# A SwiGLU FFN in seven block products: the gate of a second 1024 columns by the scheme, its up columns plain and turned

## The chip, the cores and the metric

The kernel runs on one core of a Trainium2 chip. The metric is the device time of one execution in microseconds (us), the median of several runs.

## The reference

One decoder block on 256 tokens of width 1024: a gated linear recurrence and a block-sparse attention side by side, gated, summed and projected, and then a dense SwiGLU FFN with `D_FF` = 2816. All arrays are float32. The change lies almost wholly in the last line:

```python
h2 = rmsnorm(x, ffn_norm_g[l])
x = x + (jax.nn.silu(h2 @ w_ffn_gate[l]) * (h2 @ w_ffn_up[l])) @ w_ffn_down[l]
```

`w_ffn_gate` and `w_ffn_up` are 1024 x 2816, `w_ffn_down` is 2816 x 1024. A small part of the change lies in the gate of the first branch, `sigmoid(h @ w_in[:, 7168:8192])`.

## The kernel before, in words

**Arithmetic.** Every float32 operand is split in two parts that TensorE can multiply: a high part, written by a cast on ScalarE (`whi`, line 55), and the rest, written by a subtraction on VectorE (`wlo`, line 56). One product of matrices is then three on TensorE: high by high, high by low, low by high. Weights come from memory in chunks of 1 MB (128 x 2048), each by one DMA on SyncE's queue (`load_w`, line 67, or `quarter`, line 631), and each chunk costs a cast and a subtraction of 128 x 2048. The pool `wp` that holds `wraw`, `whi` and `wlo` has three buffers of each, so the cast of a chunk can start only when TensorE has finished with the chunk three before it.

**Names.** Tokens are two blocks of 128 (index i); DFF is 22 tiles of 128 columns. `x2T` is the normalised input with the model dimension on the partitions, in high and low part. PSUM has eight banks under three tags: `pw` (4), `ph` (2), `pa` (2). In the code a quarter of a weight is `W11`, `W12`, `W21`, `W22`; in the rows below the same tiles count from zero, `W00`, `W01`, `W10`, `W11`, so that the code's `W11` is `W00` there and its `W22` is `W11`.

**Three ways to multiply by a weight.** The *plain, feature-major* way (`feat_steps`, lines 101 to 105) keeps weights stationary: for each tile of 128 columns and each of eight slices of the model dimension one matmul of 128x512 (weight's high part by high and low activations) and one of 128x256 (its low part). The sums of the two halves of a bank are then added by `fold` (ScalarE line 121, VectorE line 122). The result has the columns on the partitions, as the down projection needs it. The *token-major* way keeps the activations stationary and moves 512 columns: three matmuls of 128x512 for each slice and token block. The *scheme* (line 831) computes 2 x 2 blocks (tokens by columns, 512 deep) by seven block products instead of eight; a product (line 641) is 12 matmuls of 128x512. It needs the four quarters of a 1024 x 1024 weight, four sums of quarters (128 x 2048 each, on VectorE), sums of the activations (`token_sums2`, four arrays of 128x512, split in two pieces), and additions that put the products together. Its result is token-major, so it is turned by transposes on TensorE (`turn`, line 961: four transposes of 128x128 and a split of 128x512).

**The FFN before.** With `NPL` = 14, tiles 0 to 13 (three blocks of four and one of two) are plain and feature-major, for gate and up. Tiles 14 to 21, the last 1024 columns, go by the scheme, the gate between the chunks of the plain blocks and the up columns between the chunks of the down projection, one product and one down chunk in turn; `turn` runs four times. A down chunk (`down_steps`, lines 903 to 905) is 24 matmuls of 128x512 for two tiles; there are eleven, d0 to d10, and they add into four banks (`acc`).

**What sets the order.** The order of the steps is written out: `step` (line 795) lets nothing of a step be put ahead of the last matmul of the step before it, and a scheduler then fixes, at build time, the order on each engine. Each engine executes its own list in that order and waits at an instruction until what it needs is ready; nothing behind it overtakes.

Of the kernel before, what the change touches and what calls it, by code (L numbers as in the profile page):

```python
# [14 lines left out]
P = 128  # L15
# [12 lines left out]
def tile_hgrn2_moba_block(ctx: ExitStack, tc: tile.TileContext, xm, xw, table, runs,  # L28
# [672 lines left out]
    nc.scalar.copy(gq(1, 0), b1)  # L701
# [3 lines left out]
    at = then(product, b3, summed(0), halves(W11), True)  # L705
    W22 = quarter(1, 1, "T8")
# [16 lines left out]
    nc.vector.tensor_add(gq(1, 1), b2, gq(1, 0))
    nc.vector.tensor_add(gq(1, 1), gq(1, 1), b3)
# [55 lines left out]
    NPL = 14  # L780
    SC = NPL * P

    def token_sums2():
# [3 lines left out]
        nc.vector.tensor_add(C[:, 0], x2f[:, 0, :, P:S], x2f[:, 1, :, P:S])  # L787
        nc.vector.tensor_sub(C[:, 1], C[:, 0], x2f[:, 0, :, 0:P])
        nc.vector.tensor_sub(C[:, 2], x2f[:, 0, :, 0:P], x2f[:, 0, :, P:S])
        nc.vector.tensor_sub(C[:, 3], x2f[:, 1, :, 0:P], C[:, 1])  # L790
# [8 lines left out]
    def plain(f0, nf, b):  # L799
# [20 lines left out]
        hT = big.tile([P, nf, 2, S], F32R, name="hT", tag=("T7", "T2", "T3", "T12")[b])  # L820
# [6 lines left out]
        for j in range(nf):  # L827
            hk.append((f0 + j, hT, j))
        yield

    def scheme(w, banks, p1, at_out, q):

        X = x2T
        W11 = quarter(0, 0, "T10", w, SC)
        W21 = quarter(1, 0, "T9", w, SC)
        W12 = quarter(0, 1, "T11", w, SC)
        W22 = quarter(1, 1, "T8", w, SC)
        b1 = banks()
        product(b1, tokens(0, 0, X), halves(W11), True)
        nc.scalar.copy(p1, b1)  # L840
        nc.vector.tensor_sub(W11, W12, W11)
# [17 lines left out]
        nc.vector.tensor_sub(W21, W21, W11)
# [14 lines left out]
    def down_steps():  # L874
        (fa, act, ja), (fb, act_b, jb) = hk[2 * chunk[0]:2 * chunk[0] + 2]
        assert fb == fa + 1 and act is act_b
# [4 lines left out]
        for tb in range(2):  # L881
            for half in range(2):
                ts = slice(tb * P, (tb + 1) * P)
                cs = slice(half * 512, (half + 1) * 512)
                if end and tb == 1 and half == 1:
                    for c0, cw in ((512, 256), (768, 256)):
                        bank = pw()
                        for i in range(2):
# [10 lines left out]
                for i in range(2):  # L899
                    j = ja + i  # L900
                    st = n == 0 and i == 0
                    en = i == 1 and n == NFT // 2 - (2 if tb == 1 and half == 1 else 1)
                    nc.tensor.matmul(acc[tb][half], act[:, j, 0, ts], hi[:, i, cs], start=st, stop=False)  # L903
                    nc.tensor.matmul(acc[tb][half], act[:, j, 0, ts], lo[:, i, cs], start=False, stop=False)  # L904
                    tail[0] = nc.tensor.matmul(acc[tb][half], act[:, j, 1, ts], hi[:, i, cs], start=False, stop=en)  # L905
# [26 lines left out]
    third, chunk_no = None, 0
    for what in "cccsPcPccPcPccPcPcPc":
        if what == "c":
            with tc.issue_after(x2_split[0].ins), tc.issue_after(x2_split[1].ins):
                step(next, chunks_a) if chunk_no == 2 else None
            if chunk_no != 2:
                step(next, chunks_a)
            third = third or (halved[-1] if chunk_no == 2 else None)
            chunk_no += 1  # L940
            continue
# [106 lines left out]
```

## Time and profile before

| | |
|---|---|
| median of 3 runs | 490.17 us (490.13 to 490.63) |
| profiled execution | 490.14 us |
| its span | 488.4 us, so 1.74 us lie around it |
| TensorE busy | 483.1 us (99%), 2598 matmuls |
| VectorE busy | 397.8 us (81%), 426 instructions |
| ScalarE busy | 301.7 us (62%), 402 instructions |
| GpSimd busy | 25.2 us (5%), 59 instructions |
| granted TensorE clock | 1.00 |

The span is from the first to the last recorded instruction; the metric is somewhat longer. TensorE works almost without a gap, so its list of instructions is nearly the time. Where another engine's result comes later than TensorE's place in that list, a gap opens, and everything behind it moves. The FFN begins at about 305 us of the span.

### The profile page before, as it was taken

The numbers are of one execution on the slowest core, as the hardware profiler recorded it, in microseconds if no ns is written. First come the engines' busy times: TensorE is split into PE (matmuls) and PEld (weight loads), VectorE is DVE, ScalarE is ACT, GpSimd is POOL, SyncE is SP. The second block draws the span as 40 slices with busy tenths as digits, with TensorE's granted clock in tenths as the row PEclk, the third lists the DMA queues.
The fourth block names the chain that finished last, engine by engine and source line by source line (L and its number), as shares of the span: only waits on it lengthen the run. The fifth ranks groups of instructions, "written<-read, shape, count | busy, mean of one in ns | idle before, by whom it ended". The sixth has DMA issues, their size and how long they took to land.

```text
span 488.4 us, 6511 instructions
## 1 busy us (share of the span) xinstructions
PE 483.1 (99%) x2598; PEld 406.7 (83%) x2598; DVE 397.8 (81%) x426; ACT 301.7 (62%) x402; POOL 25.2 (5%) x59
## 2 busy tenths in 40 slices
PE   8999999999999999999999999999999999999997
PEld 7888888888888888988888878888888888888885
DVE  5769999697779989499987767899998779986843
ACT  5887656767748984875564445886566576444520
POOL 1930320000000000000000000000000000000000
PEclk9999999999999999999999999999999999999999
DMA  8977695624524348418267577715395664242402
GB/s 314 401 240 253 196 299 187 224 87 158 190 83 158 134 139 269 166 46 299 90 233 281 172 260 260 251 37 183 128 338 179 178 250 171 92 173 86 172 1 86
DMA packets 42142, 91.16 MB, mean 187 GB/s; under 512 B 1656, under 2 KB 3960, under 8 KB 42112
## 3 DMA queue, kind: packets, MB, share of 16 engines
q1 hardware_dynamic: 41376, 88.11, 52.5%
q0 software_dynamic: 736, 2.65, 1.7%
q8 instruction: 20, 0.33, 0.3%
q14 instruction: 10, 0.08, 0.1%
HBM read 89.67 MB, written 1.07 MB: 186 GB/s over the span
## 4 chain that ended last, share of the span: by engine, by line
PE 96%; DVE 2%; DMA 1%; issue 0%; ACT 0%
PE pw L102 16%; PE pw L84 10%; PE pw L85 10%; PE pw L86 10%; PE pw L168 5%; PE pw L105 4%; PE acc L903 4%; PE acc L905 4%; PE acc L904 4%; PE pw L101 4%; PE pw L645 4%; PE b L645 4%; PE g L645 3%; PE pw L684 1%; PE pw L685 1%; PE pw L683 1%
## 5 line engine op out<-in xcount | busy, mean ns | idle before, releaser
L56 DVE TENSOR_TENSOR wlo<-wraw,whi 128x2048 fp32r<-128x2048 f32 (+1 forms) x69 | 148.9, 2163 | 37.7 <-ACT whi L55 37.4
L55 ACT CAST whi<-wraw 128x2048 fp32r<-128x2048 f32 (+1 forms) x69 | 124.8, 1813 | 62.1 <-PE pw L86 25.2
L102 PE MATMUL pw<-x2T,whi 128*128 128x512 f32 x224 | 71.8, 395 | 0.0
L55 ACT CAST whi<-W 128x2048 fp32r<-128x2048 f32 x21 | 40.2, 1915 | 28.5 <-PE acc L905 13.6
L84 PE MATMUL pw<-whi,XT 128*128 128x512 f32 x144 | 56.9, 395 | 0.0
L56 DVE TENSOR_TENSOR wlo<-W,whi 128x2048 fp32r<-128x2048 f32 x21 | 47.9, 2286 | 10.2 <-ACT whi L55 10.1
L86 PE MATMUL pw<-whi,XT 128*128 128x512 f32 x144 | 56.2, 390 | 0.0
L85 PE MATMUL pw<-wlo,XT 128*128 128x512 f32 x144 | 56.1, 390 | 0.0
L102 PE MATMUL pw<-XT,whi 128*128 128x512 f32 x128 | 40.6, 395 | 0.0
L102 PEld LDWEIGHTS pw<-x2T,whi 128*128 128x128 f32 x224 | 35.0, 189 | 0.4
L86 PEld LDWEIGHTS pw<-whi,XT 128*128 128x128 f32 x144 | 27.0, 188 | 5.7
L84 PEld LDWEIGHTS pw<-whi,XT 128*128 128x128 f32 x144 | 27.0, 188 | 5.6
L105 PE MATMUL pw<-x2T,wlo 128*128 128x256 f32 x112 | 31.3, 279 | 0.3 <-DVE wlo L56 0.3
L85 PEld LDWEIGHTS pw<-wlo,XT 128*128 128x128 f32 x144 | 27.1, 188 | 5.4
L101 PE MATMUL pw<-x2T,wlo 128*128 128x256 f32 x112 | 31.2, 279 | 0.0
L105 PEld LDWEIGHTS pw<-x2T,wlo 128*128 128x128 f32 x112 | 21.1, 188 | 5.2 <-DVE wlo L56 0.7
L101 PEld LDWEIGHTS pw<-x2T,wlo 128*128 128x128 f32 x112 | 21.0, 188 | 5.0
L903 PE MATMUL acc<-whi,hT 128*128 128x512 f32 x56 | 21.9, 391 | 0.0
L905 PE MATMUL acc<-whi,hT 128*128 128x512 f32 x56 | 21.8, 390 | 0.0
L904 PE MATMUL acc<-wlo,hT 128*128 128x512 f32 x56 | 21.8, 389 | 0.0
L102 PEld LDWEIGHTS pw<-XT,whi 128*128 128x128 f32 x128 | 19.8, 189 | 0.2
L168 PE MATMUL pw<-whi,XT 128*128 128x512 f32 x64 | 17.6, 393 | 0.3 <-ACT whi L182 0.3
(357 smaller groups left out, 1019.9 us busy)
## 6 DMA issues: line engine op xcount, KB each, us to landing
wraw<-w_in SPq DMA_DIRECT2D x26, 1024.0 KB, 5.1
wraw<-w_down SPq DMA_DIRECT2D x11, 1024.0 KB, 5.0
wraw<-w_gate SPq DMA_DIRECT2D x6, 1024.0 KB, 5.1
wraw<-w_up SPq DMA_DIRECT2D x6, 1024.0 KB, 5.1
wraw<-w_at SPq DMA_DIRECT2D x4, 1024.0 KB, 6.6
W<-w_in SPq DMA_DIRECT2D x4, 1024.0 KB, 5.2
wraw<-w_hg SPq DMA_DIRECT2D x4, 1024.0 KB, 6.6
W<-w_gate SPq DMA_DIRECT2D x4, 1024.0 KB, 6.1
```

The costliest lines, as they stand in the source:

```text
L55: high = nc.scalar.copy(hi, src)
L56: return high, nc.vector.tensor_sub(lo, src, hi.bitcast(F32))
L84: nc.tensor.matmul(ps[tb], part(act, kt, 0)[:, ts], wh, start=(kt == 0), stop=False)
L85: nc.tensor.matmul(ps[tb], part(act, kt, 0)[:, ts], wl, start=False, stop=False)
L86: nc.tensor.matmul(ps[tb], part(act, kt, 1)[:, ts], wh, start=False, stop=(kt == KT - 1))
L101: nc.tensor.matmul(ps[ct][:, 0:S], lo[:, i, cs], part(act, kt, 0), start=False, stop=False)
L102: wide = nc.tensor.matmul(ps[ct], hi[:, i, cs], both, start=(kt == 0), stop=(kt == KT - 1))
L105: tail[0] = nc.tensor.matmul(ps[ct][:, 0:S], lo[:, i, cs], part(act, kt, 0), start=False, stop=False)
L168: nc.tensor.matmul(ps[tb], part(XT, kt, am)[:, tb * P:(tb + 1) * P], w[:, i, hs], start=(kt == 0 and am == 0 and w is wh), stop=(kt == KT ...
L645: mm = nc.tensor.matmul(bank, act(kt, m), h[:, kt, :], start=(first and kt == 0 and m == 0 and h is hi), stop=(kt == 3 and m == 1), skip_g ...
L903: nc.tensor.matmul(acc[tb][half], act[:, j, 0, ts], hi[:, i, cs], start=st, stop=False)
L904: nc.tensor.matmul(acc[tb][half], act[:, j, 0, ts], lo[:, i, cs], start=False, stop=False)
```

## The change

`NPL` goes from 14 to 6. Tiles 0 to 5 stay plain and feature-major. Tiles 6 to 13 (called FB) are new: their gate goes by the scheme (`GB`), their up columns by `up_plain`, the token-major way with 96 matmuls of 128x512 in four chunks (U1 to U4 below); the two are multiplied (`times`) and turned by four `turn`s. Tiles 14 to 21 (FA) keep gate and up by the scheme, but both now stand between chunks of the down projection, often two or three products in a row.

In `scheme` the signs of the sums are changed, so that products which add to the same quarter follow each other in one PSUM bank (`start=False`): `b1` takes four of the seven, and ScalarE copies its partial sum out on the way (lines 840, 850, 854). Three additions of 128x512 on VectorE are left in place of five. Two of the four activation sums become scalar_tensor_tensor; the factor −1 of the second token block's columns goes into `r2n` and into `up_scheme`. The same chaining is done in the first branch's gate (lines 698 to 735): two additions on VectorE fewer and two copies on ScalarE more, with the products in another order.

TensorE's order after, in words, with C a plain chunk, P1 to P7 the products of FB's gate, GP of FA's gate, UP of FA's up, d a down chunk, T a turn: C1 C2 C3 P1 C4 P2 C5 C6 P3 U1 P4 U2 P5 C7 C8 P6 U3 P7 T U4 T d0 T T | GP1 d1 GP2 GP3 d2 GP4 GP5 GP6 d3 GP7 | UP1 d4 UP2 UP3 UP4 d5 UP5 T UP6 T d6 T UP7 d7 T d8 d9 d10. C5 to C8 are half chunks (128 x 1024).

The diff, cut to its core:

```diff
@@ gate of the first branch
-    nc.scalar.copy(gq(1, 0), b1)
+    nc.scalar.copy(gq(0, 0), b1)
...
+    nc.scalar.copy(gq(1, 1), b3)
...
+    at = then(product, b1, summed(1), halves(W11), False)
+    nc.scalar.copy(gq(0, 1), b1)
...
-    nc.vector.tensor_add(gq(1, 1), b2, gq(1, 0))
-    nc.vector.tensor_add(gq(1, 1), gq(1, 1), b3)
+    nc.vector.tensor_add(gq(1, 1), gq(1, 1), b1)
...
-    nc.vector.tensor_add(gq(1, 0), b2, gq(1, 0))
-    sigmoid(1, 0, gq(1, 0))
+    sigmoid(1, 0, b1)
@@ FFN
-    NPL = 14
+    NPL = 6
...
@@ scheme, after
+        W11 = quarter(0, 0, "T10", w, c0)
+        W21 = quarter(1, 0, "T9", w, c0)
+        W12 = quarter(0, 1, "T11", w, c0)
+        W22 = quarter(1, 1, "T8", w, c0)
+        b1 = bank("b1")
         product(b1, tokens(0, 0, X), halves(W11), True)
+        nc.scalar.copy(q(0, 0), b1)
+        nc.vector.tensor_add(W11, W11, W12)
         yield
+        b2 = bank("b2")
+        product(b2, tokens(0, 1, X), halves(W21), True)
+        nc.vector.tensor_add(q(0, 0), q(0, 0), b2)
+        at_out(0, 0, q(0, 0))
         yield
+        b3 = bank("b3")
         product(b3, summed(0, sums2), halves(W11), True)
+        nc.scalar.copy(q(1, 1), b3)
+        nc.vector.tensor_add(W11, W11, W22)
         yield
+        product(b1, summed(1, sums2), halves(W11), False)
+        nc.scalar.copy(q(0, 1), b1)
+        nc.vector.tensor_add(W12, W12, W22)
         yield
         product(b3, summed(3, sums2), halves(W22), False)
         nc.vector.tensor_add(q(0, 1), q(0, 1), b3)
         at_out(0, 1, q(0, 1))
+        nc.vector.tensor_add(W21, W21, W11)
         yield
+        product(b1, summed(2, sums2), halves(W12), False)
+        nc.vector.tensor_add(q(1, 1), q(1, 1), b1)
+        at_out(1, 1, q(1, 1))
+        yield
+        product(b1, tokens(1, 1, X), halves(W21), False)
+        at_out(1, 0, b1)
         yield
@@ new functions
+    def up_plain(c0, q):
+        for j in range(2):
+            ps = [pw(), pw()]
+            for kt, wh, wl in chunks(w_up, c0 + j * 512, 512, (4, 4)):
+                for tb in range(2):
+                    ts = slice(tb * P, (tb + 1) * P)
+                    nc.tensor.matmul(ps[tb], part(x2T, kt, 0)[:, ts], wh, start=(kt == 0), stop=False)
+                    nc.tensor.matmul(ps[tb], part(x2T, kt, 0)[:, ts], wl, start=False, stop=False)
+                    tail[0] = nc.tensor.matmul(ps[tb], part(x2T, kt, 1)[:, ts], wh, start=False, stop=(kt == KT - 1))
...
+            for tb in range(2):
+                nc.scalar.copy(q(tb, j), ps[tb])
+            yield
+    def times(i, j):
+        nc.vector.tensor_mul(UB(i, j), UB(i, j), GB(i, j))
...
+    def up_scheme(c0, bank, q, g):
+        def at_out(i, j, src):
+            if j:
+                nc.vector.scalar_tensor_tensor(q(i, j), src, -1.0, g(i, j), op0=OP.mult, op1=OP.mult)
+            else:
+                nc.vector.tensor_mul(q(i, j), src, g(i, j))
+        return scheme(w_up, c0, bank, at_out, q)
...
@@ order of FA
+    for what in "PdPPdPPPdP":
+        step(*((down,) if what == "d" else (next, gate)))
...
+    for what in "PdPPPdP":
+        step(*((down,) if what == "d" else (next, up)))
...
+    step(turn, UA, 0, 0, *hA0, banks["b2"])
     step(next, up)
+    step(turn, UA, 0, 1, *hA1)
     step(down)
```

What the scheduler makes of it stands in the engines' lists. Three places follow. In the rows, `wlo_n` is the low part that belongs to the high part `whi` with the number just below.

**First place: VectorE, between the second and the third gate product.** Before:

```order
L853 TENSOR_TENSOR W01_2797<-W11_2799,W01_2797 128x2048
L56 TENSOR_TENSOR hT_2859<-zt_2727,hT_2859 128x2x256
L825 TENSOR_TENSOR zt_2727<-zt_2727,fl_2858 128x512
L56 TENSOR_TENSOR wlo_2935<-wraw_2933,whi_2934 128x2048
L56 TENSOR_TENSOR hT_2859<-zt_2727,hT_2859 128x2x256
L56 TENSOR_TENSOR wlo_2986<-W00_2793,whi_2985 128x2048
L56 TENSOR_TENSOR wlo_3008<-wraw_3006,whi_3007 128x2048
L122 TENSOR_TENSOR zt_2971<-pw_2891,zt_2971 128x256
L122 TENSOR_TENSOR zt_2971<-pw_2892,zt_2971 128x256
L122 TENSOR_TENSOR zt_2971<-pw_2893,zt_2971 128x256
```
After, where `wlo_2950` is the third product's weight and `wlo_2972` that of the first chunk of `up_plain`:

```order
L845 TENSOR_TENSOR GB_2648<-GB_2648,b2_2876 128x512
L855 TENSOR_TENSOR W01_2799<-W01_2799,W11_2801 128x2048
L56 TENSOR_TENSOR hT_2861<-zt_2729,hT_2861 128x2x256
L56 TENSOR_TENSOR wlo_2950<-W00_2795,whi_2949 128x2048
L122 TENSOR_TENSOR zt_2941<-pw_2895,zt_2941 128x256
L122 TENSOR_TENSOR zt_2941<-pw_2896,zt_2941 128x256
L851 TENSOR_TENSOR W00_2795<-W00_2795,W11_2801 128x2048
L810 TENSOR_TENSOR zt_2941<-zt_2941,R2_2636 128x512
L56 TENSOR_TENSOR wlo_2972<-wraw_2970,whi_2971 128x2048
```
The split of the third product's weight stood behind a whole plain chunk's split and ahead of another plain chunk's; now it is followed by two folds, a weight sum (line 851), a multiplication, and only then by the split for the step that comes directly after the third product.

**Second place: VectorE, from the fourth down chunk to the up scheme's fourth product.** Before, where `wlo_3564` and `wlo_3612` are weights of up products, with `wlo_3534`, `wlo_3582` and `wlo_3630` of down chunks between them:

```order
L56 TENSOR_TENSOR wlo_3534<-wraw_3532,whi_3533 128x2048
L56 TENSOR_TENSOR hT_3462<-zt_3408,hT_3462 128x2x256
L56 TENSOR_TENSOR wlo_3564<-W10_3507,whi_3563 128x2048
L853 TENSOR_TENSOR W01_3509<-W11_3511,W01_3509 128x2048
L56 TENSOR_TENSOR wlo_3582<-wraw_3580,whi_3581 128x2048
L56 TENSOR_TENSOR wlo_3612<-W00_3505,whi_3611 128x2048
L959 TENSOR_TENSOR U_3562<-pw_3513,sG_2646 128x512
L848 TENSOR_TENSOR W00_3505<-W11_3511,W00_3505 128x2048
L56 TENSOR_TENSOR wlo_3630<-wraw_3628,whi_3629 128x2048
L859 TENSOR_TENSOR W10_3507<-W10_3507,W00_3505 128x2048
```
After, where the two rows just ahead are the split of d3's weight (`wlo_3475`) and an addition of 128x512 (line 858), `wlo_3504` is the weight of GP7, `wlo_3531`, `wlo_3580`, `wlo_3599` and `wlo_3617` are those of UP1 to UP4, and `wlo_3550` is d4's:

```order
L56 TENSOR_TENSOR wlo_3504<-W10_3295,whi_3503 128x2048
L863 TENSOR_TENSOR GA_3292<-GA_3292,b1_3301 128x512
L56 TENSOR_TENSOR wlo_3531<-W00_3521,whi_3530 128x2048
L841 TENSOR_TENSOR W00_3521<-W00_3521,W01_3525 128x2048
L855 TENSOR_TENSOR W01_3525<-W01_3525,W11_3527 128x2048
L56 TENSOR_TENSOR wlo_3550<-wraw_3548,whi_3549 128x2048
L56 TENSOR_TENSOR wlo_3580<-W10_3523,whi_3579 128x2048
L56 TENSOR_TENSOR wlo_3599<-W00_3521,whi_3598 128x2048
L851 TENSOR_TENSOR W00_3521<-W00_3521,W11_3527 128x2048
L860 TENSOR_TENSOR W10_3523<-W10_3523,W00_3521 128x2048
L845 TENSOR_TENSOR UA_3520<-UA_3520,b2_3578 128x512
L56 TENSOR_TENSOR wlo_3617<-W00_3521,whi_3616 128x2048
```
The splits of UP2, UP3 and UP4 now stand with no down chunk's split between them, and two weight sums (lines 851 and 860) come right ahead of UP4's.

**Third place: the end of the up scheme.** VectorE before, where `wlo_3792` is the last product's weight and `wlo_3811` that of the down chunk behind it:

```order
L856 TENSOR_TENSOR U_3562<-pw_3659,p1u_3474 128x512
L56 TENSOR_TENSOR wlo_3792<-W10_3507,whi_3791 128x2048
L857 TENSOR_TENSOR U_3562<-U_3562,pw_3610 128x512
L959 TENSOR_TENSOR U_3562<-U_3562,sG_2646 128x512
L56 TENSOR_TENSOR wlo_3811<-wraw_3809,whi_3810 128x2048
L862 TENSOR_TENSOR U_3562<-U_3562,pw_3610 128x512
L56 TENSOR_TENSOR wlo_3855<-wraw_3853,whi_3854 128x2048
L959 TENSOR_TENSOR U_3562<-U_3562,sG_2646 128x512
L56 TENSOR_TENSOR hq1_3765<-turn_3784,hq1_3765 128x4x128
```
VectorE after, where `wlo_3718` is d6's weight and `wlo_3753` that of UP7:

```order
L56 TENSOR_TENSOR wlo_3718<-wraw_3716,whi_3717 128x2048
L858 TENSOR_TENSOR UA_3520<-UA_3520,b3_3597 128x512
L56 TENSOR_TENSOR wlo_3753<-W10_3523,whi_3752 128x2048
L934 SCALAR_TENSOR_TENSOR UA_3520<-UA_3520,GA_3292 128x512
L56 TENSOR_TENSOR hq_3684<-b2_3578,hq_3684 128x4x128
L863 TENSOR_TENSOR UA_3520<-UA_3520,b1_3529 128x512
L56 TENSOR_TENSOR hq_3683<-turn_3709,hq_3683 128x4x128
```
TensorE before, where `turn_3784` reads the quarter `U(1,1)`, for which the additions of lines 856 and 857 and the multiplication behind them (line 959) are the last steps:

```order
L645 MATMUL pw_3610<-whi_3766,C2h_2783 128x512
L645 MATMUL pw_3610<-wlo_3767,C2h_2783 128x512
L645 MATMUL pw_3610<-whi_3766,C2l_2784 128x512
L965 MATMUL turn_3784<-ident_268,U_3562 128x128 x4
L645 MATMUL pw_3659<-whi_3791,x2T1_2460 128x512
```
TensorE after, where `b1` with `whi_3691` is the end of UP6 and `whi_3717` belongs to d6:

```order
L645 MATMUL b1_3529<-whi_3691,C2h_2785 128x512
L645 MATMUL b1_3529<-wlo_3692,C2h_2785 128x512
L645 MATMUL b1_3529<-whi_3691,C2l_2786 128x512
L960 MATMUL turn_3709<-ident_268,UA_3520 128x128 x4
L902 MATMUL acc00_3242<-whi_3717,hh_3276 128x512
L903 MATMUL acc00_3242<-wlo_3718,hh_3276 128x512
```
The quarter `UA(0,1)` is finished by the addition of line 858 and the multiplication of line 934; the split of d6's weight stands ahead of both on VectorE's list, and that of UP7's between them. The quarter needs UP5, and between UP5 and its turn stand on TensorE another turn and UP6; before, a product and a whole down chunk stood between the fifth product and the turn of `U(1,1)`.

More of the change, by code (lines that the diff above doesn't have):

```diff
@@ L933, in tile_hgrn2_moba_block @@
[L933 to L941, printed above, removed]
-        with tc.issue_after(third[0].ins), tc.issue_after(third[1].ins):
-            if what == "P":
-                step(next, gate)
-            else:
-                sums2 = token_sums2()
@@ L947, in tile_hgrn2_moba_block @@
-    assert not list(chunks_a) and not list(gate)
-    rest = plain(12, 2, 3)
-    for _ in range(4):
-        step(next, rest)
-    U = None
-    hq = [None, None]
-    def uq(i, j):
-        return U[:, i, j * 512:(j + 1) * 512]
-    def hidden(i, j, src):
-        nc.vector.tensor_mul(uq(i, j), src, gq2(i, j))
-    def turn(i, j):
-        bank = pw("turn")
-        src = uq(i, j)
-        for k in range(4):
-            tail[0] = nc.tensor.transpose(bank[:, k * P:(k + 1) * P], src[:, k * P:(k + 1) * P], ident)
-        ts = slice(i * P, (i + 1) * P)
-        split(bank.rearrange("p (k t) -> p k t", k=4), hq[j][:, :, 0, ts], hq[j][:, :, 1, ts])
+    r2n = small.tile([P, 2], F32, name="r2n")
@@ new lines, in times, with turn, turned @@
+    def times(i, j):
+        nc.vector.tensor_mul(UB(i, j), UB(i, j), GB(i, j))
+    def turn(q, i, j, hi, lo, bank=None):
+        bank = bank or pw("turn")
+        for k in range(4):
+            tail[0] = nc.tensor.transpose(bank[:, k * P:(k + 1) * P], q(i, j)[:, k * P:(k + 1) * P], ident)
+        ts = slice(i * P, (i + 1) * P)
+        split(bank.rearrange("p (k t) -> p k t", k=4), hi[:, :, ts], lo[:, :, ts])
+    def turned(f0, tags):
+        t = [big.tile([P, 4, S], F32R, name="hh", tag=g) for g in tags]
+        for k in range(4):
+            hk.append((f0 + k, lambda m, ts, k=k: t[m][:, k, ts]))
+        return t
@@ new lines, in turned2 @@
+    def turned2(f0, tag):
+        t = big.tile([P, 2, 4, S], F32R, name="hq", tag=tag)
+        for k in range(4):
+            hk.append((f0 + k, lambda m, ts, k=k: t[:, m, k, ts]))
+        return t[:, 0], t[:, 1]
+    FB, FA = NPL, NPL + 8
+    GB = quarters("GB", "T6")
+    ring = iter([pa, ph, pa])
+    gate = gate_scheme(FB * P, lambda name: next(ring)(name), GB)
+    first_c, second_c = plain(0, 4, 0), plain(4, 2, 1)
+    for k in range(2):
+        step(next, first_c)
+    with tc.issue_after(x2_split[0].ins), tc.issue_after(x2_split[1].ins):
+        step(next, first_c)
@@ new lines, in tile_hgrn2_moba_block @@
+    third = halved[-1]
+    with tc.issue_after(third[0].ins), tc.issue_after(third[1].ins):
+        sums2 = token_sums2()
+        step(next, gate)
+        step(next, first_c)
+        step(next, gate)
+    step(next, second_c)
+    step(next, second_c)
+    step(next, gate)
+    UB = quarters("UB", "T7")
+    up_b = up_plain(FB * P, UB)
+    step(next, up_b)
+    step(next, gate)
+    step(next, up_b)
+    step(next, gate)
+    times(0, 0)
+    step(next, second_c)
+    step(next, second_c)
@@ L969, in tile_hgrn2_moba_block @@
+    step(next, gate)
+    step(next, up_b)
+    step(next, gate)
+    times(1, 0)
+    hB0 = turned2(FB, "T3")
+    step(turn, UB, 0, 0, *hB0)
+    step(next, up_b)
+    assert not list(up_b) and not list(gate) and not list(first_c) and not list(second_c)
+    times(0, 1)
+    times(1, 1)
+    step(turn, UB, 1, 0, *hB0)
     acc = [[ph("acc00"), ph("acc01")], [pa("acc10"), pa("acc11")]]
-    p1u = big.tile([P, 512], F32, name="p1u", tag="T15")
-    up = scheme(w_up, pw, p1u, hidden, uq)
     step(down)
+    hB1 = turned(FB + 4, ("T13", "T15"))
@@ L987, in tile_hgrn2_moba_block @@
[L987 to L988 removed]
+    step(turn, UA, 1, 1, *hA1, banks["b3"])
     step(next, up)
     assert not list(up)
[L991 to L1001 removed]
+    step(down)
+    step(turn, UA, 1, 0, *hA0, banks["b2"])
+    for _ in range(3):
```

122 lines of the change are left out of this document (42 added, 80 removed).

## The prediction

> **What bounds the kernel now.** I read the page first: the span, the busy shares, the share of the chain by engine.
>
> ```profile
> span 488.4 us, 6511 instructions
> PE 483.1 (99%) x2598; PEld 406.7 (83%) x2598; DVE 397.8 (81%) x426; ACT 301.7 (62%) x402; POOL 25.2 (5%) x59
> PE 96%; DVE 2%; DMA 1%; issue 0%; ACT 0%
> ```
>
> TensorE (PE) is busy 99% and carries 96% of the chain. Then I read the view of waits. Its rows for PE say that PE almost never stood still for another engine:
>
> ```profile
> PE warm L156 <- DVE ones L151: 1.1, 1, 1.1
> PE pw L105 <- DVE wlo L56: 0.3, 1, 0.3
> PE pw L168 <- ACT whi L182: 0.3, 1, 0.3
> ```
>
> So every matmul removed is worth its issue interval, as long as the other engines go on hiding. How near they are to not hiding is told by the windows (length, then busy time and count of PE, PEld, DVE, ACT and POOL, then the granted clock, DMA share and GB/s), taken over the FFN's three stages and the start:
>
> ```profile
> 305.00:345.00 40.00, 39.70 (x223) 34.13 (x223) 38.08 (x44) 29.88 (x38) 0.00 (x0) 1.00 0.48 158
> 345.00:405.00 60.00, 60.00 (x326) 51.69 (x325) 51.00 (x52) 38.12 (x45) 0.00 (x0) 1.00 0.63 213
> 405.00:456.00 51.00, 51.00 (x230) 42.07 (x230) 42.67 (x29) 26.00 (x17) 0.00 (x0) 1.00 0.34 121
> 0.00:2.00 2.00, 0.88 (x4) 0.88 (x5) 0.86 (x2) 1.20 (x1) 0.78 (x6) 1.00 0.18 19
> ```
>
> In the first 40 us of the FFN VectorE (DVE) has 38.08 busy: it is nearly a second bound, just where the change starts to rearrange it. The later stages have 15% free. DMA moves at half its share or little above it, and the clock is 1.00 throughout.
>
> **TensorE, removed and added.** From the chain, products (L645) with their start and duration:
>
> ```profile
> 331.80 2.72 PE g L645 x12
> 345.67 2.72 PE g L645 x12
> 409.30 2.72 PE pw L645 x12
> 417.46 2.72 PE pw L645 x12
> 433.78 2.72 PE pw L645 x12
> 442.38 2.77 PE pw L645 x12
> ```
>
> A product is 2.72 us, 0.2267 for each of its 12 matmuls. From 409.30 to 417.46, 8.16 us, stand a product and a down chunk of 24 matmuls: 5.44, the same 0.2267 each. From 331.80 to 345.67, 13.87, stand a product and two plain chunks of 16 pairs (128x512 and 128x256): 11.15/32 = 0.348 a pair. Between 433.78 and 442.38 a turn stands beside product and down chunk: 8.60 − 8.16 = 0.44.
>
> Removed: eight tiles, each with eight pairs for gate and eight for up, 128 pairs × 0.348 = 44.60. Added: seven products (84 matmuls) and `up_plain` (96), 180 × 0.2267 = 40.80, and four turns, 1.76. The gain on PE is 44.60 − 40.80 − 1.76 = **2.04 us**. Chaining in PSUM changes no matmul count. That is the whole gain; what follows are waits.
>
> **VectorE, in sum.** Step lengths, from start to next start, come from the timeline:
>
> ```profile
> 309.53 2.29 DVE L56 TENSOR_TENSOR wlo<-wraw,whi 128x2048 fp32r<-128x2048 f32 x1 [1.11 <-ACT whi L55]
> 311.81 0.67 DVE L787 TENSOR_TENSOR C<-x2f 128x512 f32<-128x512 f32 x1
> 312.40 0.68 DVE L789 TENSOR_TENSOR C<-x2f 128x512 f32<-128x512 f32 x1
> 320.03 1.22 DVE L56 TENSOR_TENSOR C2l<-C,C2h 128x1024 fp32r<-128x1024 f32 x1
> 321.16 2.28 DVE L841 TENSOR_TENSOR W<-W,W 128x2048 f32<-128x2048 f32 x1
> 328.90 0.41 DVE L122 TENSOR_TENSOR fl<-pw,fl 128x256 f32<-128x256 f32 x1
> 329.24 2.28 DVE L56 TENSOR_TENSOR wlo<-wraw,whi 128x2048 fp32r<-128x2048 f32 x1
> ...
> 339.24 2.28 DVE L56 TENSOR_TENSOR wlo<-W,whi 128x2048 fp32r<-128x2048 f32 x1
> 342.12 2.29 DVE L56 TENSOR_TENSOR wlo<-wraw,whi 128x2048 fp32r<-128x2048 f32 x1 [0.60 <-ACT whi L55]
> ...
> 424.45 2.28 DVE L56 TENSOR_TENSOR wlo<-wraw,whi 128x2048 fp32r<-128x2048 f32 x1
> 426.65 2.28 DVE L859 TENSOR_TENSOR W<-W,W 128x2048 f32<-128x2048 f32 x1
> 428.86 2.28 DVE L56 TENSOR_TENSOR wlo<-W,whi 128x2048 fp32r<-128x2048 f32 x1
> ```
>
> A split or weight sum of 128x2048 is 2.20 in a row of work (424.45 to 426.65) and 2.29 to its end; 128x1024 is 1.13 (320.03 to 321.16), 128x512 0.60, a fold of 128x256 0.34. Beyond the folds and multiplications of eight plain tiles, which go (about −15 us), come four weight sums, three more whole splits, and the additions, multiplications and lows of four turns (about +21): near +6 us over 180, which the 15% free would take. What counts is the order.
>
> **Wait 1, the third gate product and `up_plain`'s first chunk.** Before, DVE worked from 309.53 without a gap to 341.52 (339.24 + 2.28, the third product's split): 31.99 us, and the product began at 345.67, 4.15 later. After, the same stretch has two whole splits fewer (−4.40), two half ones (+2.26), one addition (+0.60), `r2n` and the longer scalar_tensor_tensor (+0.23): 30.68, so 340.21. PE is one chunk shorter there (16 pairs, 5.57), and the product is due at 340.10. Until here nearly nothing is lost; but `up_plain` comes directly behind it, and its first split stands behind two folds, the sum of line 851 and a multiplication: 0.68 + 2.20 + 0.60 + 2.29 = 5.77, ready at 345.98. PE needs it after the product and two matmuls, 340.10 + 2.72 + 0.45 = 343.27. The wait is 2.7; with a gap on DVE such as the 0.60 before 342.12, which a late cast opens, 3.3. I take 2.9. Below, the cover would have to be 2.7 longer, and nothing on DVE in that stretch is shortened by so much.
>
> **Wait 2, d2.** Its split stands behind two sums, an addition and a product's split, all started only when GP1 has freed its buffer. By the same steps it comes 0 to 0.3 late; I take 0.2.
>
> **Wait 3, UP4.** A cast starts right where PE leaves the buffer: PE's last matmul of a product ends at 420.18, the cast begins at 420.21.
>
> ```profile
> 419.79 0.39 PE L645 MATMUL pw<-whi,x2T 128*128 128x512 f32 x1
> 420.21 1.92 ACT L55 CAST whi<-wraw 128x2048 fp32r<-128x2048 f32 x1 [0.80 <-PE pw L645]
> L840 ACT COPY p1u<-pw 128x512 f32<-128x512 f32 x1 | 0.6, 587 | 0.7 <-PE pw L645 0.7
> L908 DVE SCALAR_TENSOR_TENSOR x<-acc,r,x 128x512 f32<-128x512 f32 x3 | 2.3, 751 | 1.8 <-PE acc L905 1.8
> ```
>
> After, d3's cast has to wait for GP4 and stands behind ScalarE's copy of `b1`: from d2's end 2.72 + 0.17 (the last matmul's tail) + 0.50 + 1.92 = 5.31 until DVE may split it. From there DVE has ten whole operations, three of 128x512 and UP4's split: 22.00 + 1.80 + 2.29 = 26.09, in all 31.40. PE has GP4 to GP6, d3, GP7, UP1, d4, UP2 and UP3, 7 × 2.72 + 2 × 5.44 = 29.92, and 0.23 to the first use of the low part: 30.15. The wait is 1.25. In that stretch PE offers two down chunks to hide seven products' weights, and three sums stand there besides.
>
> **Wait 4, the turn of UA(0,1).** From d5's end: the tail 0.17, d6's cast 1.92, its split 2.20, the addition 0.60, UP7's split 2.20, the scalar_tensor_tensor 0.75 (751 ns on line 908): 7.84. PE has UP5, a turn and UP6: 5.88. The wait is 1.96, and d6, the last turns and all down chunks behind it move along.
>
> The waits do not cancel one another: after each, PE is late and DVE has gained, but the next count starts anew where a freed buffer lets a cast begin.
>
> For all four waits a rule can be weighed on the rows 424.45 and 426.65. The Trainium skill, "VectorE: DVE Perf Modes", section "Terms", calls DRAIN a flush after every operation, so that "next op can't issue until 8-slice pipe empties". By it the next operation would start at 424.45 + 2.28 = 426.73 at the earliest; the trace has 426.65. Taken strictly it would add 0.08 to each of some 36 operations ahead of wait 1, 2.9 us, and the forecast would be about 497; but before's own stretch would then have ended 2.6 us later than it did, so the measurement decides, the rule gets no chance of its own, and I keep 2.20.
>
> **Queues and the rest at nothing.** The first branch's gate loses two additions and gains two copies of 0.6 on ScalarE; the chunks of 24 matmuls (5.44) around each of them are the cover, and if it fails, one copy is the price. The chaining binds a product to ScalarE's copy of its bank; at P4 and P6 another step of 2.72 or more lies between. SyncE's queue: the quarters of the later schemes are fetched into tiles that are freed by a split; the nearest row is
>
> ```profile
> W<-w_gate SPq DMA_DIRECT2D x4, 1024.0 KB, 6.1
> ```
>
> 6.1 us to landing. For FA's up weight W10, which may be fetched only after GP7's split, that is just when UP2's cast wants it: 0 to 1 us, and DVE is then still busy with the splits ahead. I take 0. GpSimd's queue has nothing in the FFN.
>
> **Sum.** Waits 2.9 + 0.2 + 1.25 + 1.96 = 6.3, less 2.04: +4.3 on the profiled execution's 490.14, that is 494.4. That execution is within 0.03 of the median 490.17, so the same stands for it.
>
> **Rivals.**
> - *DVE keeps ahead (the other side).* If DVE reached `up_plain`'s first split 2.7 us sooner and had as much over at UP4 and UP6, only PE's gain would be left: 490.14 − 2.04 = 488.1. For it speaks that DVE's total in the FFN is under PE's; against it the 38.08 of 40 and the listed order. It decides from a DVE lead of 4.3 us in sum. 7%.
> - *Half the waits.* The splits are 5% faster or casts start earlier: +1.1, 491.3 (to 493). 7%.
> - *The clock drops in the gaps.* Waits of 2 to 3 us have no equal in this trace; at half clock a product costs 2.72 more: once 497.1, behind each of three waits 502.6. Against it stands the clock of 1.00 in the first 2 us, though PE idled 1.1 there. 5%. (The Trainium skill, "TensorE: Matmul & The Clock Gate", section "Part 1: The HAM clock gate (the "warmup" mystery)", throttles after an idle window of about 3.4 us, which a wait of 2.9 would not fill; no row here shows a gap that long.)
> - *A quarter lands late.* One or two of the quarters take 1 to 3 us longer than 6.1, as DMA already has 0.63 in the middle stage: 496 to 498. 8%.
>
> **How the numbers follow.** The forecast has 73%, with its own range 492.5 to 495.5 from the ends of the terms and half a us for casts. The range leaves out the rival that ends faster and the clock, 12%, and reaches over the other two: 491.5 to 497.5. A difference of 0.2%, 1 us, is about what a measurement of this kernel can tell from no change. Faster 0.07; within it 0.03, from the weakest of the half waits; slower 0.90.
>
> **What would show it.** In the profile after, PE's waits should name `wlo` (L56) at `up_plain`'s first chunk with 2.7 to 3.3 us, at UP4 with about 1.2, and a turn waiting for a product of line 934 with about 2; PE's busy time should be some 2 us lower. I am wrong if DVE's third-product split ends well before 340, if PE waits for ScalarE's copies, or if the granted clock shows less than 1.00.

## The result, and the profile after

The changed kernel takes 497.84 us (median of 4 runs, 496.56 to 498.25) against 490.33 us before; the ratio is 1.0148, 95% interval 1.0128 to 1.0168. It is slower, as forecast, but by 7.5 us and not by 4.3, and 0.3 us outside the range. The profiled execution took 496.56 us at a granted clock of 1.000, 6.42 us more than the profiled one before. The other three runs had a mean granted clock of 0.997 and took 497.65 to 498.25; this second part of the loss is taken apart below.

The page of the changed kernel, the same lines as before:

```profile
span 494.9 us, 6389 instructions
PE 482.9 (98%) x2538; PEld 402.9 (81%) x2538; DVE 403.9 (82%) x411; ACT 308.6 (62%) x402; POOL 24.9 (5%) x59
PE 88%; DVE 8%; ACT 1%; issue 1%; DMA 1%; DVEq 0%
```

DVE has 6.1 us more to do, as forecast, and has entered the chain with 8%. The view of waits names the places:

```profile
PE pw L946 <- DVE wlo L56: 2.4, 1, 2.4
PE b L645 <- DVE wlo L56: 2.3, 2, 1.4
PE turn L960 <- DVE UA L934: 1.8, 1, 1.8
PE warm L156 <- DVE ones L151: 1.1, 1, 1.1
PE acc L903 <- DVE wlo L56: 0.5, 1, 0.5
```

These are the four forecast places: `up_plain`'s first chunk (L946), a gate product and UP4 (both L645), the turn of UA(0,1) (L960) and d2 (L903). What such a wait costs is seen in the timeline of PE, from start to start:

```profile
339.54 0.40 PE L645 MATMUL b<-whi,C2h 128*128 128x512 f32 x1
340.88 0.50 PE L645 MATMUL b<-wlo,C2h 128*128 128x512 f32 x1 [0.95 <-DVE wlo L56]
...
343.51 0.61 PE L945 MATMUL pw<-whi,x2T 128*128 128x512 f32 x2
346.55 0.50 PE L946 MATMUL pw<-wlo,x2T 128*128 128x512 f32 x1 [2.42 <-DVE wlo L56]
...
405.40 1.07 PE L902 MATMUL acc<-whi,hT 128*128 128x512 f32 x4
406.95 0.50 PE L903 MATMUL acc<-wlo,hT 128*128 128x512 f32 x1 [0.48 <-DVE wlo L56]
...
430.65 1.07 PE L902 MATMUL acc<-whi,hq 128*128 128x512 f32 x4
431.77 0.50 PE L903 MATMUL acc<-wlo,hq 128*128 128x512 f32 x1
...
441.88 0.39 PE L645 MATMUL b<-whi,C2h 128*128 128x512 f32 x1
443.62 0.50 PE L645 MATMUL b<-wlo,C2h 128*128 128x512 f32 x1 [1.35 <-DVE wlo L56]
...
457.39 0.39 PE L645 MATMUL b<-whi,C2l 128*128 128x512 f32 x1
459.58 0.66 PE L960 MATMUL turn<-ident,UA 128*128 128x128 f32 x4 [1.80 <-DVE UA L934]
```

From 441.88 to 443.62 are 1.74 us where 0.23 would do, 1.5 lost, while the row lists 1.35. The idle time shown begins at the end of the last matmul, whose tail of 0.17 runs beside the next one when nothing waits. Besides, the matmul behind a gap starts its successor about 0.11 later. From the start of one block to the start of the next (the ends are starts of rows not shown) the losses are 1.25 at the third product (339.54 to 343.51, 3.97 for a block of 2.72), 2.74 at `up_plain` (to 351.69, 8.18 for 5.44), 0.78 at d2 (405.40 to 411.62, 6.22 for 5.44), 0.35 at d4 (430.65 to 436.44; its row at 431.77 lists no gap), 1.65 at UP4 (441.88 to 446.25) and 1.95 at the turn: 8.7 us.

The last matmuls, before and after, close the account:

```profile
483.39 1.44 PE pw L891 x12
```

```profile
489.81 1.44 PE pw L891 x12
```

6.42 us later. Of that 0.2 lies ahead of the FFN; 0.6 that the fourth chunk lost before (6.17 for 5.57, with the 0.3 of `pw L105`) is gone. So PE's own list is 8.7 + 0.2 − 0.6 − 6.4 = 1.9 us shorter, where 2.04 was forecast.

### The profile page after: what moved, and what is told of

It reads as the page before. It is cut to its first block, busy times and chain, and to the rows that moved or that the text cites. A ratio compares the mean times of both kernels' runs of the same rounds, so it can differ in the third digit from the quotient of the medians.

```text
span 494.9 us, 6389 instructions
## 1 busy us (share of the span) xinstructions
PE 482.9 (98%) x2538; PEld 402.9 (81%) x2538; DVE 403.9 (82%) x411; ACT 308.6 (62%) x402; POOL 24.9 (5%) x59
## 4 chain that ended last, share of the span: by engine, by line
PE 88%; DVE 8%; ACT 1%; issue 1%; DMA 1%; DVEq 0%
PE b L645 10%; PE pw L102 10%; PE pw L84 10%; PE pw L85 10%; PE pw L86 10%; PE pw L168 5%; DVE wlo L56 5%; PE acc L903 3%; PE acc L904 3%; PE acc L902 3%; PE pw L101 2%; PE pw L105 2%; PE pw L946 2%; PE pw L947 1%; PE pw L683 1%; PE pw L685 1%
## 5 line engine op out<-in xcount | busy, mean ns | idle before, releaser
L55 ACT CAST whi<-W 128x2048 fp32r<-128x2048 f32 x28 | 53.6, 1913 | 27.5 <-PE acc L904 6.9
L56 DVE TENSOR_TENSOR wlo<-W,whi 128x2048 fp32r<-128x2048 f32 x28 | 63.8, 2287 | 7.0 <-ACT whi L55 6.8
L102 PE MATMUL pw<-x2T,whi 128*128 128x512 f32 x96 | 31.0, 396 | 0.0
L645 PE MATMUL b<-whi,x2T 128*128 128x512 f32 x72 | 23.7, 392 | 0.0
L645 PE MATMUL b<-wlo,C2h 128*128 128x512 f32 x48 | 18.9, 394 | 2.3 <-DVE wlo L56 2.3
L645 PE MATMUL b<-whi,C2h 128*128 128x512 f32 x48 | 18.8, 392 | 0.0
L645 PE MATMUL b<-whi,C2l 128*128 128x512 f32 x48 | 18.7, 390 | 0.0
L903 PE MATMUL acc<-wlo,hq 128*128 128x512 f32 x46 | 18.0, 392 | 0.0
L904 PE MATMUL acc<-whi,hq 128*128 128x512 f32 x46 | 17.9, 389 | 0.0
L101 PE MATMUL pw<-XT,wlo 128*128 128x256 f32 x64 | 17.8, 278 | 0.0
L105 PE MATMUL pw<-XT,wlo 128*128 128x256 f32 x64 | 17.8, 277 | 0.0
```

Source lines behind the costliest of these rows:

```text
L55: high = nc.scalar.copy(hi, src)
L56: return high, nc.vector.tensor_sub(lo, src, hi.bitcast(F32))
L101: nc.tensor.matmul(ps[ct][:, 0:S], lo[:, i, cs], part(act, kt, 0), start=False, stop=False)
L102: wide = nc.tensor.matmul(ps[ct], hi[:, i, cs], both, start=(kt == 0), stop=(kt == KT - 1))
L105: tail[0] = nc.tensor.matmul(ps[ct][:, 0:S], lo[:, i, cs], part(act, kt, 0), start=False, stop=False)
L645: mm = nc.tensor.matmul(bank, act(kt, m), h[:, kt, :], start=(first and kt == 0 and m == 0 and h is hi), stop=(kt == 3 and m == 1), skip_g ...
```

## The experiments

**The sum of line 851 behind the split that PE waits for.** In the first scheme only:

```diff
         nc.scalar.copy(q(1, 1), b3)
-        nc.vector.tensor_add(W11, W11, W22)
-        yield
+        yield
+        with tc.issue_after(halved[-1][1].ins):
+            nc.vector.tensor_add(W11, W11, W22)
```

> The changed kernel (497.84 us) with one move: the weight sum of line 851 of the first scheme stands on VectorE behind the split of up_plain's first chunk, not ahead of it. Theory 'order' (only the row in front costs): the wait of 2.74 us at up_plain's first chunk goes and nothing comes for it, 495.1. Theory 'supply' (VectorE is simply out of time in this stage): the wait moves to the fourth product, whose weight is that sum, with about 2.0 us, and the time falls by 0.7 only, 497.1. Clock: three of four runs of the changed kernel had a mean granted clock of 0.997 and were 1.1 to 1.7 us longer; if the 2.4 us gap sets that off, a longest gap of 2.0 may leave 1.000, and 1.3 us more go.

Measured: 496.01 us (495.75 to 496.32), clock 0.999 to 1.000 in all four runs. The timeline of PE shows where the wait went:

```profile
351.45 0.50 PE L645 MATMUL b<-wlo,C2h 128*128 128x512 f32 x1 [1.71 <-DVE wlo L56]
```

`up_plain` no longer waits, and the fourth product does, with 1.71. Against the changed kernel's run at full clock, 496.56, it is 0.5 us less (0.2 against 496.17, the full-clock run of its second measurement below): "supply" held, not "order". Taking one row out of the way moves a wait when DVE has no time left at that place. The other 1.3 us, to the changed kernel's median, come from the clock.

**Every gate product of the first scheme one step later.** The steps ahead of d0:

```diff
     with tc.issue_after(third[0].ins), tc.issue_after(third[1].ins):
         sums2 = token_sums2()
-        step(next, gate)
-        step(next, first_c)
-        step(next, gate)
+    step(next, first_c)
+    step(next, gate)
...
-    times(1, 0)
-    step(turn, UB, 1, 0, *hB0)
...
+    step(next, gate)
+    times(1, 0)
...
+    step(turn, UB, 1, 0, *hB0)
```

> The changed kernel with the gate products of the first scheme one TensorE step later each (C1 C2 C3 C4 P1 C5 C6 P2 U1 P3 U2 P4 C7 C8 P5 U3 P6 T U4 P7 d0 T T T), so VectorE has 5.5 us more before each. Theory 'supply': of the 4 us of waits at the third product and up_plain's first chunk about 1 us is left, at the second product; 497.84 - 3.2 = 494.6 with the clock as in the changed kernel, 493.3 with a granted clock of 1.000 in all runs, since the two gaps close together are gone. Rival 'TensorE' (the loss lies in the new instructions themselves, since TensorE's busy time fell by 0.2 us only): no change, 497.8.

Measured: 492.90 us (492.58 to 493.53), clock 0.999 to 1.000 in all four runs. The waits of PE:

```profile
PE b L645 <- DVE wlo L56: 2.2, 2, 1.4
PE turn L960 <- DVE UA L934: 1.8, 1, 1.8
```

At the first place 0.87 us is left, at the second product; UP4's 1.37 and the turn's 1.80 are untouched. 4.9 us came back against the changed kernel's median, 3.7 of them against its run at full clock (496.56); d2's wait went with the rest. So the loss at the first place was that the products began before DVE could keep up, not their instructions.

**The turn of UA(0,1) behind d6.**

```diff
     step(next, up)
-    step(turn, UA, 0, 1, *hA1)
     step(down)
+    step(turn, UA, 0, 1, *hA1)
     step(turn, UA, 1, 1, *hA1, banks["b3"])
```

> The changed kernel with the turn of UA(0,1) behind the sixth down chunk, d6, instead of ahead of it. Theory: the wait of 1.95 us at that turn goes, 0.4 comes back at the next turn, -1.6: 496.2. Rival: the quarter is late for the down chunk that reads it in any place, and the wait only moves: 497.8. Clock: the gaps at the third product and up_plain stay, so a mean granted clock of 0.997 in most runs if they set it off; 1.000 if the gap at the turn does, and then 494.9.

Measured: 494.45 us in one run, at a clock of 0.999, and 496.11, 496.44 and 496.68 in three at 0.995 to 0.996. Each group is 1.6 to 2.1 below its counterpart of the changed kernel: wait 4 was real and did not come back elsewhere. The two groups stay, so this gap is not what lowers the clock.

**The up scheme with a down chunk ahead of its fourth product.**

```diff
-    for what in "PdPPPdP":
+    for what in "PdPPdPP":
```

> The changed kernel with the up scheme as P d P P d P P T P, so that a down chunk stands ahead of the fourth product and the turn of UA(0,1) follows on UP6 as before the move. Theory: the waits at d4 and UP4 (0.35 and 1.65) shrink to about 0.2, at the turn 1.0 is left in place of 1.95: 2.7 less than the changed kernel, 493.8 in a run of full clock and 495.3 in one of 0.997, which stay as frequent since place one is as it was. Rival: as in the move of the sum at the first place, the wait only goes to a neighbour: 497.

Measured: 493.40 us at clock 1.000, and 494.93, 495.23 and 495.29 at 0.997: 0.4 under the expectation in the one case and 0.1 in the other. The wait at UP4 is gone, 0.68 is left at the turn. Here, later in the FFN, DVE had time, and order alone was missing.

**All moves of order together.** The later gate products, the up scheme as P d P P d P P, and the turn behind d6:

> The changed kernel with the same instructions in another order: gate products of the first scheme one step later each (as in the run before), the up scheme as P d P P d P P T d T T P, so that its fourth product has a down chunk ahead of it and the turn of UA(0,1) stands behind d6. Theory 'order' (the work fits, it only stands wrongly): the waits fall from 8.7 to about 1.7 us, the granted clock is 1.000 or 0.999 in all runs, and TensorE's gain of 1.9 us shows: 489.8, 0.5 under the kernel before. Rival 'supply' (VectorE is short of time over the whole FFN): waits come back at other places with 4 us or more in sum, 492.5.

Measured: 489.74 us (489.05 to 489.97, 11 runs), ratio to before 0.9985, interval 0.9977 to 0.9994. PE's only wait in the FFN:

```profile
PE b L645 <- DVE wlo L56: 0.9, 1, 0.9
```

With the same instructions the kernel is 0.5 us under the 490.26 of the kernel before in these rounds, and 8.1 us under the changed one. Start to start, the waits left in its trace cost about 1.5 us (1.14 at the second product, 0.31 at a down chunk) where the changed kernel lost 8.7. PE's gain was there; the order had hidden it. "Supply" as a bound over the whole FFN is refuted. As a bound on what can be begun in the first 40 us it stands: DVE is busy there for 38.25 of 40 in this run too.

**The same with line 855's sum one step later in each scheme.**

```diff
         nc.scalar.copy(q(0, 1), b1)
-        nc.vector.tensor_add(W12, W12, W22)
         yield
+        with tc.issue_after(halved[-1][1].ins):
+            nc.vector.tensor_add(W12, W12, W22)
```

> The best order so far (489.74 us) with the weight sum of line 855 one step later in each scheme, behind the next product's split. Theory: the wait of 0.9 us at the second gate product goes; d2 and d5 wait 0.6 and 0.6 in place of 0.2 and 0.2, 489.6. Rival 'supply': the sum is only late elsewhere, 489.7 to 490.

Measured: 489.76 us (489.05 to 490.04, 11 runs), ratio to before 0.9989, interval 0.9980 to 0.9998. The wait of 0.9 went and two of 0.5 came, at d2 and a later down chunk. No gain over the order before.

**Two of the four sums on GpSimd.** In the best order:

```diff
-        nc.vector.tensor_add(W12, W12, W22)
+        nc.gpsimd.tensor_add(W12, W12, W22)
...
-        nc.vector.tensor_add(W21, W21, W11)
+        nc.gpsimd.tensor_add(W21, W21, W11)
```

> The same order, and two of the four weight sums of each scheme (lines 855 and 860) on GpSimd in place of VectorE. Theory: VectorE loses six operations of 2.2 us, the rest of the waits (1.4 us) goes, and GpSimd's sums have time enough: 488.4. Rival: VectorE's operations are longer beside a GpSimd sum, or GpSimd's sum is over 8 us long and a product's cast waits for it: 490 to 493.

Measured: 501.77 us (500.71 to 502.49), 12 us more than the same order on VectorE alone. The timelines of POOL and of DVE:

```profile
327.96 4.60 POOL L855 TENSOR_TENSOR W<-W,W 128x2048 f32<-128x2048 f32 x1 [84.25 <-DMA wraw<-w_up]
349.76 6.44 POOL L860 TENSOR_TENSOR W<-W,W 128x2048 f32<-128x2048 f32 x1 [17.20 <-PE pw L947]
```

```profile
328.40 4.70 DVE L824 TENSOR_TENSOR zt<-zt,fl 128x512 f32<-128x512 f32 x1
349.44 2.28 DVE L56 TENSOR_TENSOR wlo<-wraw,whi 128x2048 fp32r<-128x2048 f32 x1
351.67 6.67 DVE L56 TENSOR_TENSOR wlo<-W,whi 128x2048 fp32r<-128x2048 f32 x1
```

A multiplication of 0.68 us lasts 4.70 when it starts beside a GpSimd sum, and ends 0.54 after it; a split of 2.28 lasts 6.67. The two engines do not share, one stands still: a sum of 2.2 us taken off VectorE costs it 4.0 and 4.4 in these rows. The clock fell in three of these four runs, but the fourth took 501.26 at 1.000, so it is not the cause. The Trainium skill, "SBUF — State Buffer", section "SBUF: two separate sides", says that GpSimd and a VectorE operation with two inputs in SBUF hold one port pair in turn, for the whole instruction; the rows agree.

**The chaining alone.** The kernel before, with `NPL` = 14 and its own order, and the new `scheme`, signs and first branch's gate; the last product stands inside the down chunk behind it:

```diff
+        b2 = bank("b2")
+        product(b2, tokens(0, 1, X), halves(W21), True)
+        nc.vector.tensor_add(q(0, 0), q(0, 0), b2)
...
+        product(b1, summed(1, sums2), halves(W11), False)
+        nc.scalar.copy(q(0, 1), b1)
```

> The kernel before (490.33 us), NPL = 14 and its order of steps, with the chained sums alone: signs, b1 used four times, three additions in place of five and two copies more on ScalarE, in both schemes and in the first branch's gate; the last product stands inside the down chunk behind it. Theory (costed at nothing): TensorE's list is the same, VectorE's work less, 490.3 within 0.5 us. Rival: a product has to wait for ScalarE's copy or VectorE's addition on its bank; with three such places in each of three schemes at 0.6 us each, up to +5, 495; half of that is 492.8.

Measured: 490.45 us (10 runs), ratio 1.0002, interval 0.9993 to 1.0012. Costed at nothing, and it is nothing; the copies are no part of the loss.

**The clock, by one gap in the kernel before.** In `load_w` VectorE does the split of one down chunk `again` times more, which makes PE stand once:

```diff
+            for _ in range(again):
+                nc.vector.tensor_sub(lo[:, i:i + n, :], raw[:, i:i + n, :], hi[:, i:i + n, :].bitcast(F32))
...
-        hi, lo = load_w(w_down[...], [2, D])
+        hi, lo = load_w(w_down[...], [2, D], 1, 4 if n == 10 else 0)
```

> The kernel before (490.33 us) with one gap: the split of the last down chunk is done five times over on VectorE (the same result each time), so TensorE stands once for about 2.5 us, 5 us ahead of the end. Theory 'clock': a gap alone of this length lowers the clock in most runs: mean 0.996 to 0.998, bimodal times, 492.8 and up to 494.5. Rival: it takes the two gaps of 1.1 and 2.7 us behind one another that the changed kernel has; then 492.8 in all runs, clock 0.999 to 1.000.

The second has `3 if n == 8 else 0`:

> The kernel before with one gap of about 3.3 us, at the ninth down chunk, whose split is done four times over; 16 us of TensorE work follow. Theory 'clock': if a gap of 2.5 does not lower the clock, this one does, in most runs: 493.6 without, 495 to 496 with a mean clock of 0.996. Rival: a lone gap never does it: 493.6 in all runs, 0.999 to 1.000.

Measured: with a gap of 2.4 us 493.10 and 493.54 at clock 1.000, 494.63 and 495.01 at 0.997; with one of 3.0 us 493.88 and 493.91 at 1.000, 494.67 and 495.05 at 0.996 to 0.997. A lone gap does it, in two of four runs each. The profiled run of the first was one of those; its windows, behind the gap that ends at 482.66:

```profile
480.00:483.00 3.00, 0.62 (x4) 0.38 (x3) 2.61 (x2) 0.00 (x0) 0.00 (x0) 1.00 0.00 0
483.00:486.00 3.00, 3.00 (x10) 2.32 (x9) 0.75 (x1) 0.00 (x0) 0.00 (x0) 0.59 0.00 0
```

**The changed kernel once more.**

> The changed kernel once more, for its clock. A lone gap of 2.4 us lowered the clock in two of four runs, and the trace of one shows matmuls of 0.43 us in place of 0.227 for 3.4 us behind the gap. If the gap of 2.4 us at up_plain's first chunk does the same here, two or three of four runs have a mean clock of 0.997 and about 498.0 us, the others 496.5; where the profiled one is among the first, its windows show the lower clock right behind 346.5 us and not elsewhere. Rival: the low clock lies at another place, the turn's gap of 1.8 or the start.

Measured: 498.07 us, of its four runs one 496.17 at clock 1.000 and three 498.06 to 498.24 at 0.997; the profiled one was at 1.000, so it does not show the place. The profile of the kernel with the spread up scheme, whose first stage is the same, does. Its windows at `up_plain`'s first chunk (the gap ends at 346.30), and its matmuls there:

```profile
343.00:346.30 3.30, 0.88 (x4) 0.38 (x4) 3.30 (x4) 2.84 (x4) 0.00 (x0) 1.00 0.00 0
346.90:350.20 3.30, 3.30 (x9) 2.64 (x8) 3.30 (x2) 1.27 (x1) 0.00 (x0) 0.50 0.58 159
350.30:353.00 2.70, 2.70 (x13) 2.23 (x12) 2.55 (x2) 0.00 (x0) 0.00 (x0) 1.00 0.43 85
```

```profile
346.30 0.50 PE L946 MATMUL pw<-wlo,x2T 128*128 128x512 f32 x1 [2.42 <-DVE wlo L56]
346.64 0.43 PE L947 MATMUL pw<-whi,x2T 128*128 128x512 f32 x1
346.87 0.63 PE L946 MATMUL pw<-wlo,x2T 128*128 128x512 f32 x1
347.30 0.63 PE L947 MATMUL pw<-whi,x2T 128*128 128x512 f32 x1
...
350.28 0.39 PE L945 MATMUL pw<-whi,x2T 128*128 128x512 f32 x1
350.51 0.39 PE L946 MATMUL pw<-wlo,x2T 128*128 128x512 f32 x1
```

From 346.87 on, 0.57 after the gap's end, the clock is 0.50 for 3.4 us: eight matmuls at 0.427 in place of 0.227, 1.6 us. That is about the distance between the two groups of runs. Of the 16 runs of kernels with this gap (the changed one twice, the turn behind d6, the spread up scheme) 12 were in the group of low clock; where the longest gap was 1.80, in the sum's and the later products' kernels, none of eight.

Which runs it hits can be read from the traces too, since each holds the record of the granted clock. In all 13 the clock changes only on a grid of 3.41 us, whose start differs from run to run (3.97 to 6.67 us into the span). Where TensorE was idle for 2.18 us or more of one cell of the grid at full clock, the next cell was at 0.50; after 1.93 or less it stayed at 1.00. The gap of 2.42 above lay in one cell, 343.44 to 346.86. The profiled run with the gap of 3.0 and that of the changed kernel's second measurement kept the full clock, and in both a border of the grid cut the gap (length, then PE's busy time; the clock is the third figure from the end):

```profile
468.22:471.63 3.41, 1.56 (x7) 0.94 (x6) 3.41 (x3) 1.91 (x1) 0.00 (x0) 1.00 0.00 0
471.63:475.05 3.42, 2.30 (x10) 1.92 (x11) 3.27 (x2) 0.00 (x0) 0.00 (x0) 1.00 0.00 0
```

```profile
342.18:345.59 3.41, 1.48 (x7) 0.90 (x5) 3.41 (x3) 2.35 (x3) 0.00 (x0) 1.00 0.00 0
```

Length less PE's busy time leaves 1.85 and 1.12 us idle in the first two, and 1.93 in the third. A mean clock of 0.998 or 0.999, which runs of the kernel before show too, need not cost time: in the profile of the best order (0.999) the only record of 0.50 begins at 486.56, and TensorE's last matmul ends at 484.08.

## Why the prediction was wrong

**What held.** The direction, all four places with their engine, PE's gain (2.04 forecast, 1.9 found), wait 4 (1.96 and 1.95), the chaining, first branch and queues at nothing, and VectorE's 6 us more (6.1). That DVE keeps ahead was the wrong rival, as its 38.08 of 40 had said.

**What failed.** Two steps. Waits 1 to 3 were sized too low: 4.35 us were taken, 6.2 measured, with the 0.6 at the fourth chunk set against them. And the sum took a drop of the clock at nothing; it came in three of four runs and put the median outside the range.

**Wait 1 was sized 0.5 too low.** 2.9 was taken, 1.25 + 2.74 = 4.0 measured, 3.4 when the 0.6 at the fourth chunk is set against it. The third product was due at 339.54 and not at 340.10: the 0.6 that the chunk lost before is lost no more, and 345.67, from which the count started, is a row of the chain, which begins at the end of the matmul before; in the timeline the product starts at 345.50. The FFN's start, 0.2 later, takes a part back. DVE ended its split at 338.55 + 2.29 = 340.84 and not at 340.21: it had the gap that the upper bound spoke of, a cast that came late:

```profile
332.80 1.23 DVE L56 TENSOR_TENSOR wlo<-wraw,whi 128x1024 fp32r<-128x1024 f32 x1 [0.52 <-ACT whi L55]
...
338.55 2.29 DVE L56 TENSOR_TENSOR wlo<-W,whi 128x2048 fp32r<-128x2048 f32 x1
```

The end of the range, 3.3, was near; the value inside it was not.

**Waits 2 and 3 were sized 1.3 too low.** 0.2 + 1.25 were taken; 0.78 at d2, 0.35 at d4 and 1.65 at UP4 were measured. The last two are one count, wait 3's from d2's end to UP4, and d4 is no term left out. Over half of the difference is the step of 2.20, which holds for operations that have nothing to do with one another. DVE's rows from UP1's split to UP4's, without a gap:

```profile
422.57 2.28 DVE L56 TENSOR_TENSOR wlo<-W,whi 128x2048 fp32r<-128x2048 f32 x1
424.89 2.29 DVE L841 TENSOR_TENSOR W<-W,W 128x2048 f32<-128x2048 f32 x1
427.22 2.29 DVE L855 TENSOR_TENSOR W<-W,W 128x2048 f32<-128x2048 f32 x1
429.43 2.29 DVE L56 TENSOR_TENSOR wlo<-wraw,whi 128x2048 fp32r<-128x2048 f32 x1
431.63 4.49 DVE L56 TENSOR_TENSOR wlo<-W,whi 128x2048 fp32r<-128x2048 f32 x2
436.15 2.29 DVE L851 TENSOR_TENSOR W<-W,W 128x2048 f32<-128x2048 f32 x1
438.48 2.29 DVE L860 TENSOR_TENSOR W<-W,W 128x2048 f32<-128x2048 f32 x1
440.69 0.68 DVE L845 TENSOR_TENSOR UA<-UA,b 128x512 f32<-128x512 f32 x1
441.28 2.28 DVE L56 TENSOR_TENSOR wlo<-W,whi 128x2048 fp32r<-128x2048 f32 x1
```

From sum to sum it is 2.33 (lines 841 to 855, lines 851 to 860), and 2.32 from UP1's split to the sum that overwrites the tile it read; from a sum to an unrelated operation it is 2.21. In each long step the second operation shares a tile with the first that one of them writes. Four of the ten steps of wait 3 are of this kind, 0.5 us in all, and two ahead of d2's split, 0.25. I had put the rule of a pipe that empties first aside on the evidence of two unrelated operations; between dependent ones 0.1 is indeed paid. The rest is small: a matmul starts 0.06 after the split that it waits for has ended (443.56 and 443.62 at UP4), about 0.14 more is lost at the matmuls behind each gap, and d2's own count, 0 to 0.3, was taken in its middle.

These two waits and wait 1, 1.8 us, and 0.2 ahead of the FFN explain the profiled run: 494.4 + 2.0 = 496.4 of 496.56, and the rest is PE's gain of 1.9 in place of 2.04.

**The rival on the clock was set aside too easily.** It had 5%; it came in three of the four runs and adds 1.3 to the median, which puts the time outside the range. The step that failed is its evidence, the clock of 1.00 beside 1.1 us of idleness at the start. That 1.00 was not measured: the first record of the clock in the trace before begins at 4.12 us, and the view shows 1.00 where there is none. A row of the same trace says otherwise:

```profile
1.12 3.47 PE L156 MATMUL warm<-ones 128*128 128x128 f32 x16 [1.12 <-DVE ones L151]
```

Sixteen matmuls of 128x128 in 3.47 us are 0.22 each, where a turn's four take 0.44, 0.11 each: TensorE began at half its speed. "At half clock a product costs 2.72 more" was also off: 1.6, since the low clock lasts 3.4 us. The Trainium skill, "TensorE: Matmul & The Clock Gate", section "Part 1: The HAM clock gate (the "warmup" mystery)", gives 3.4 us for the window and half the clock, and both agree with the eight matmuls of 0.427; that a whole idle window must pass first does not: gaps of 2.4 us lowered it, and 2.18 us idle in one cell of the grid were enough.

**"PE's busy time some 2 us lower"** was a poor sign: it fell by 0.2 only, because at each of six waits the modelled tail of 0.17 no longer overlaps and the matmul behind the gap counts 0.11 more. The steps of the blocks show the gain, the busy sum does not.

## What to carry to other kernels

Where one engine is the bound and a second is busy for 95% of a stage, count the second's queue at each place where the first reads from it, start to start, before paying for a gain on the first with work on the second. If moving one row only moves the wait, delay the consumer as a whole, here by one chunk; with the two other moves of order the kernel then ended 0.5 us under the kernel before. A gap on TensorE of 2.4 us or more should be priced with about 1.6 us more, paid here in half to three quarters of the runs. And a clock of 1.00 in a view is evidence only where the trace has a record of it.

## What the runs showed of the hardware that was not expected

- A TensorE gap of 2.4 us is enough to halve the clock for 3.4 us; gaps up to 1.8 us were not, in eight runs. Whether it happens depends on where the gap lies on a grid of 3.41 us that starts at another time in each run: 2.18 us or more idle in one cell brought the low clock in the next, 1.93 or less did not, in 13 traces. Between the two figures no cell was seen.
- A 128x2048 sum on GpSimd (4.60 us) holds up VectorE's whole next operation, from 0.68 to 4.70 us, and waits in turn for one that is under way (6.44).
- VectorE's step is 2.20 us between unrelated 128x2048 operations and 2.32 to 2.33 between dependent ones.
